# Expert layer: six buffers for row numbers, remainder tokens fetched as half rows, scatter-adds that skip empty slots

## The chip, the cores and the metric

The kernel runs on one core of a Trainium2 chip. A core has five engines that run in parallel, each with its own queue of instructions in program order: TensorE (PE: matmuls and transposes; PEld is its weight load), VectorE (DVE), ScalarE (ACT), GpSimd (POOL) and SyncE (SP, which here issues most DMAs). Sixteen DMA engines move data between DRAM and the on-chip memory SBUF. Indirect DMAs, whose rows are picked by a list of row numbers, are issued from POOL. The metric is the device time of one execution in microseconds.

## The reference, cut to what matters

One decoder layer for 1024 tokens with 1024 channels, in float32: token mixing by attention and a recurrence, cross-attention into 256 memory tokens, and a mixture of experts. Only the last part is changed:

```python
def grouped_moe(x, router_w, router_bias, w_gate, w_up, w_down):
    s = sigmoid(x @ router_w)                      # 16 experts in 4 groups of 4
    group = argmax(sum of the best two of s + router_bias in each group)
    e_idx = top_k(s + router_bias inside that group, 2)
    gate = s[e_idx] / sum(s[e_idx])
    # tokens sorted by expert, each expert's rows through
    y_rows = (silu(xb @ w_gate[e]) * (xb @ w_up[e])) @ w_down[e]   # 1024 -> 512 -> 1024
    return segment_sum(y_rows * gate, token)
x = layer_norm(DN_ALPHA * x + grouped_moe(x, ...), ln3_g, ln3_b)
```

With two experts to a token there are 2048 assignments. Which tokens an expert gets is known only while the kernel runs.

## The kernel before, in words

**Precision.** Each float32 operand of a large product is split into a high and a low part (`Ctx.split`, line 28: a cast on ACT, then a subtraction on DVE), and a product is three matmuls (`mm3`, lines 35 to 37): high x high, low x high, high x low.

**Lists.** The router writes, for every expert, a region of rows (token, 1, gate) in DRAM. An expert has 128 main slots (`CAP`); the eight experts with the most tokens (`NREM`) have 64 more (`REM`), their remainder. An empty slot's row is all zero. A loop behind the stage (`rest`) serves tokens past these slots.

**An expert.** Its weights come in six pieces of 1 MB (`load`, L1508, issued by SP), which are split by `parts`: the cast on ACT (L1517), the subtraction (L1518) for three of four parts on DVE, for one on POOL. `rows` (L1527 to L1535) loads 128 list rows `el` by SP and makes of them, on POOL, the tile `ef` (token, gate and intermediate values; `f` in the code) and the tile `eix` (`ix`: column 0 the row to read, column 1 the row to add to, which for an empty slot is a row past the tokens). `ef` and `eix` have three buffers each, for main lists and for remainders separately, so a fourth expert's list waits until the first one's last reader is done; for `eix` this is the scatter-add. `gather` (L1540) fetches the tokens' 1024 channels by an indirect DMA from `x2d` into `exg`. `turned` (L1547) transposes them, eight 128x128 transposes for 128 rows, into two banks of PSUM, which `split` turns into the stationary operand. For a remainder the 64 tokens are fetched twice, to both halves of the partitions, so that after the transposition 64 columns hold the high parts and 64 the low parts (`exr`).

The products with `w_gate` and `w_up` go through PSUM (`eacc`); for a remainder these are the matmuls of L1580. The hidden values are turned (L1547 for main tokens, `etq` L1599 for a remainder), multiplied (L1602, L1603 on DVE) and split (`ehh`, `ehl`; `ehr` for a remainder), and the product with `w_down` follows (lines 35 to 37; L1628 and L1629 for a remainder). ACT scales by the gate (L1616), and POOL adds the result to the sum `acc` in DRAM (`accd`) by an indirect DMA that accumulates (L1621): one of 128 rows for main tokens, two of 64 for a remainder. Every addition to `acc` waits for the one before it. The rows past the tokens (T to T + 127) take what empty slots give.

**Order.** `run` interleaves the stages of neighbouring experts: lists and main tokens of expert n + 2 are opened between the stages of n and n + 1, the remainder of n + 1 is fetched at the end. Experts with and without a remainder alternate from the second on. The queues' final order is a planner's, which simulates the engines and puts ready instructions first. The two experts at the end (`LATE`) fetch the sum so far, normalise their tokens and write them to the output by indirect DMAs with a bound on the row number (L1624). All other outputs come from `tiles` (L1757 to L1763), which loads `acc` by tiles, applies the last layer norm and stores.

Of the kernel before, what the change touches and what calls it, by code (L numbers as in the profile page):

```python
# [7 lines left out]
F32 = mybir.dt.float32  # L8
F32R = mybir.dt.float32r
I32 = mybir.dt.int32  # L10
AF = mybir.ActivationFunctionType
ALU = mybir.AluOpType
# [3 lines left out]
T, D = 1024, 1024  # L16
# [41 lines left out]
def load_xT(k, pool, ps, xin, ident, xh, xl, nt=NT, tag="xraw", bufs=3, pt=(("tp", 2),)):  # L58
    """four token tiles at a time: their loads, then their transposes"""
# [22 lines left out]
class Inproj:  # L82
    """x @ w_in; every consumer's layout goes to DRAM scratch."""
# [40 lines left out]
    # weights stationary, channels on the partitions  # L124
# [5 lines left out]
    def halves(self, wh, wl, evac, tag=None, marks=()):  # L130
        """a half of the tokens at a time"""
# [15 lines left out]
    def tokens(self, x, w, nh):  # L147
        """four token tiles by channels, from channels by tokens"""
        tp = self.bank(nh, "iptp")
        for i in range(4):  # L150
            self.k.nc.tensor.transpose(tp[:, w * i:w * i + w], x[:, 128 * i:128 * i + 128], self.ident[:w, :w])
        return tp[:, :4 * w]
# [112 lines left out]
def t5_onehot():  # L265
    """bucket of distance 1023 - i, one-hot (columns past distance 0 stay empty)"""
# [11 lines left out]
def bias_rows(k, pool, ev, ps, skew):  # L278
    """the bias by distance in DRAM, a copy for every partition; read with rows one place shorter, row p starts p places earlier"""
# [16 lines left out]
class Tables:  # L296
    """bias tables by distance: tb[p, h, c]: distance p + 896 - c; tcm: the compressed keys'; the window's far edge"""
# [24 lines left out]
def compress(k, cst, pool, ps):  # L322
    """k_cmp (twice on the partitions, in parts) and v_cmp (tokens on the partitions, in parts)"""
# [68 lines left out]
class Nsa:  # L392
    def __init__(self, k, cst, dp, skew, ps, keep, right):
        """first loads and the compressed branch's keys and values; ps: a pool with banks for that; keep: opens a pool that stays"""
# [33 lines left out]
    def load(self, t, g, half):  # L428
        """by halves of the tokens"""
# [10 lines left out]
    def attention(self):  # L440
# [6 lines left out]
        with tc.tile_pool(name="nq", reuse_waits="tile", bufs=1) as self.pq, tc.tile_pool(name="nw", reuse_waits="tile", bufs=2) as pw, tc.tile_pool(name="np", reuse_waits="tile", bufs=2, space=PSUM) as ps:  # L447
            def front(br, g, qt, t, st):
                """scores, softmax and gates of one tile of 128 queries of a group"""
# [28 lines left out]
            def weights(g, qt, sums, bs):  # L478
                """the gates over the sums"""
# [7 lines left out]
            def compressed(g, qt, t, st):  # L487
                """scores, softmax and gates against the compressed keys, four heads at once"""
# [20 lines left out]
            def back(g, qt, t, st):  # L509
                """all three branches into one sum: channels of four heads by queries"""  # L510
# [37 lines left out]
            def mix(a, na, b, nb):  # L548
                """steps of a among the first ones of b"""
# [71 lines left out]
class Rwkv:  # L621
    """RWKV-7 in chunks of 64 tokens; an item is a pair of heads and half of the tokens.

    Per chunk, with c the running sum of the log decay: al = e^{c_prev} kk, be = e^{-c} kk a, ka = e^{-c} k, rho = e^{c} r;
    U = (I + tril(al be^T, -1))^{-1} (al S^T + tril(al ka^T, -1) V); outputs and the next state are linear in S, U and V."""
# [37 lines left out]
    def low_rank(self):  # L663
        """the low-rank inputs past their nonlinearities, to DRAM"""
# [14 lines left out]
    def item(self, hp, n):  # L679
        """an item up to its maps, the end of the one before, the item's recurrence"""  # L680
# [12 lines left out]
    def steps(self, hp, n):  # L693
# [33 lines left out]
        # decay and in-context rate  # L727
# [12 lines left out]
        # normalised removal key  # L740
# [15 lines left out]
        # chunk operands: [al | rho | e^c at the chunk's end on a diagonal], and be, ka as a pair per chunk (swapped in odd chunks)  # L756
# [21 lines left out]
        # bonus  # L778
# [5 lines left out]
        # within the chunks  # L784
# [19 lines left out]
        # tokens on the partitions  # L804
# [22 lines left out]
        # inverses of the diagonal blocks of 32, a block to a partition  # L827
# [4 lines left out]
        # X (I + L^T) = I by rows: partition (row group of 8, block), a step clears one column to the right  # L832
# [16 lines left out]
        # (I + L)^-1 [al | L V], over both chunks of a unit  # L849
# [21 lines left out]
        # one map per chunk from the state to outputs and the next state  # L871
# [29 lines left out]
        # group norm, bonus, gate  # L901
# [34 lines left out]
EARLY = 4  # products of the merge during the attention before it  # L936
# [965 lines left out]
```

## Time and profile before

| what | value |
|---|---|
| runs, us | 1888.84, 1890.29, 1898.58 (median 1890.29) |
| profiled execution: span, us (its own time is given by this span alone) | 1889.9 |
| PE busy over the span | 1763.5 us, 93% |
| DVE busy | 1323.7 us, 70% |
| ACT busy | 849.3 us, 45% |
| POOL busy | 670.3 us, 35% |
| indirect and other POOL-issued DMAs (q0) | 26.62 MB, 5.7% of 16 engines' span |
| DMAs issued by SP (q1) | 273.59 MB, 44.7% |

The experts' matmuls begin at 1417.49 us of the span. Until 1444 the first expert runs almost alone, from 1444 to 1830 neighbouring experts overlap, and from 1830 on the last products, the last norm and the stores follow. Busy time is what an engine spent in instructions. A wait is put down to the instruction or DMA that released it. In the timeline a row has the start, the length in us, the engine, the line, the operation, output<-input, and in square brackets the idle time before it and what ended that.

### The profile page before, as it was taken

The page shows a single profiled execution, that of the slowest core. Times are in us where ns is not written, and L with a number is a line of the kernel's source. Part 1 is how long each engine was busy: PE and PEld are TensorE (multiplying, and loading weights), DVE is VectorE, ACT ScalarE, POOL GpSimd, SP SyncE. Part 2 cuts the span into 40 slices and gives each one's busy share as a digit, 9 for nine tenths or more (in the row PEclk, how much of TensorE's full clock was granted, in tenths as well). Part 3 has the DMA queues.
Part 4 walks back from the last instruction along what each step waited for, and adds up shares of the span by engine and source line. Part 5 has one row for each costly group of instructions (what it writes and reads, how often), then busy time and mean ns, then how long its engine had stood idle before and what let it go on. Part 6 is the DMA issues. An engine that isn't in the chain of part 4 may idle for free. (4 is left out here: it accounts for less than half of the span.)

```text
span 1889.9 us, 27421 instructions
## 1 busy us (share of the span) xinstructions
PE 1763.5 (93%) x9206; PEld 1433.0 (76%) x9206; DVE 1323.7 (70%) x2774; ACT 849.3 (45%) x1742; POOL 670.3 (35%) x756
## 2 busy tenths in 40 slices
PE   8999999999999999999999899999998999999992
PEld 6877777777788887877888577878796887787771
DVE  3225886888887512498987675557888788788876
ACT  4223313434333222287876341034415676666662
POOL 1123202221222122155445122100356665666556
PEclk9999999999999999999999999999989999999996
DMA  7363343444332227702101774033326999899984
GB/s 232 110 186 106 116 162 113 140 122 126 101 113 84 67 89 231 256 9 82 40 9 32 236 221 167 23 98 126 137 84 246 310 331 289 278 295 292 320 269 143
DMA packets 246144, 302.00 MB, mean 160 GB/s; under 512 B 54653, under 2 KB 142741, under 8 KB 245488
## 3 DMA queue, kind: packets, MB, share of 16 engines
q1 hardware_dynamic: 238016, 273.59, 44.7%
q0 software_dynamic: 7984, 26.62, 5.7%
q8 instruction: 74, 1.21, 0.3%
q14 instruction: 70, 0.57, 0.1%
HBM read 234.05 MB, written 70.98 MB: 161 GB/s over the span
## 5 line engine op out<-in xcount | busy, mean ns | idle before, releaser
L1518 DVE TENSOR_TENSOR wlo<-wraw,whi 128x512 fp32r<-128x512 f32 x288 | 274.5, 1000 | 34.9 <-ACT whi L1517 33.9
L35 PE MATMUL acc<-xh,wh 128*128 128x512 f32 (+1 forms) x656 | 273.0, 416 | 5.2 <-ACT wh L117 3.0
L37 PE MATMUL acc<-xh,wl 128*128 128x512 f32 (+1 forms) x656 | 267.0, 408 | 0.1
L36 PE MATMUL acc<-xl,wh 128*128 128x512 f32 (+1 forms) x656 | 267.1, 408 | 0.0
L1517 ACT CAST whi<-wraw 128x512 fp32r<-128x512 f32 x384 | 207.4, 621 | 36.5 <-PE eacc L1580 10.1
L118 POOL TENSOR_TENSOR wl<-wraw,wh 128x1024 fp32r<-128x1024 f32 (+1 forms) x41 | 104.0, 2536 | 304.1 <-ACT wh L117 259.8
L35 PEld LDWEIGHTS acc<-xh,wh 128*128 128x128 f32 (+1 forms) x656 | 125.0, 191 | 44.0 <-issue 6.8
L1518 POOL TENSOR_TENSOR wlo<-wraw,whi 128x512 fp32r<-128x512 f32 x96 | 138.8, 1476 | 49.4 <-ACT whi L1517 38.1
L37 PEld LDWEIGHTS acc<-xh,wl 128*128 128x128 f32 (+1 forms) x656 | 124.8, 190 | 33.8 <-issue 5.1
L36 PEld LDWEIGHTS acc<-xl,wh 128*128 128x128 f32 (+1 forms) x656 | 125.2, 191 | 30.0 <-issue 3.2
L840 DVE TENSOR_TENSOR tinv<-xinv,ln 128x248 f32<-128x248 f32 (+30 forms) x248 | 85.5, 345 | 40.5 <-DMA ln<-ld 24.3
L28 DVE TENSOR_TENSOR pl<-ptp,ph 128x512 fp32r<-128x512 f32 (+1 forms) x148 | 98.3, 681 | 11.6 <-ACT ph L28 11.1
L470 ACT ACTIVATE pp<-pp,nm 128x640 f32<-128x640 f32 (+7 forms) x128 | 94.2, 738 | 16.4 <-DVE nm L469 15.6
L28 ACT CAST ph<-ptp 128x512 fp32r<-128x512 f32 (+1 forms) x148 | 84.7, 582 | 26.6 <-PE ptp L523 23.6
L36 PE MATMUL eacc<-wlo,exh 128*128 128x512 f32 x240 | 94.2, 393 | 0.4 <-DVE wlo L1518 0.4
L35 PE MATMUL eacc<-whi,exh 128*128 128x512 f32 x240 | 94.3, 393 | 0.0
L37 PE MATMUL eacc<-whi,exl 128*128 128x512 f32 x240 | 94.1, 392 | 0.0
L841 DVE TENSOR_TENSOR xinv<-xinv,tinv 128x248 f32<-128x248 f32 (+30 forms) x248 | 87.6, 353 | 5.9
L475 POOL TENSOR_SCALAR pp<-pp,wgt 128x640 f32<-128x640 f32 (+7 forms) x128 | 88.9, 717 | 1.0
L969 POOL TENSOR_SCALAR lnrs<-lnmv 128x1 f32<-128x1 f32 x21 | 19.6, 934 | 181.0 <-DVE lnmv L968 173.1
L523 PE MATMUL ptp<-ident,pp 128*128 128x128 f32 x528 | 82.1, 278 | 0.3 <-DVE pl L28 0.3
L117 ACT CAST wh<-wraw 128x1024 fp32r<-128x1024 f32 (+1 forms) x41 | 42.2, 1030 | 81.8 <-PE acc L36 44.4
(498 smaller groups left out, 4476.2 us busy)
## 6 DMA issues: line engine op xcount, KB each, us to landing
wraw<-in_moe_w_up SPq DMA_DIRECT2D x32, 1024.0 KB
wraw<-in_moe_w_gate SPq DMA_DIRECT2D x32, 1024.0 KB
wraw<-in_moe_w_down SPq DMA_DIRECT2D x32, 1024.0 KB
wraw<-in_w_in SPq DMA_DIRECT2D x40, 512.0 KB
sm<-ev SPq DMA_DIRECT2D x32, 256.0 KB
sr<-ev SPq DMA_DIRECT2D x28, 256.0 KB
skew<-skew SPq DMA_DIRECT2D x1, 4608.0 KB
xraw<-in_x SPq DMA_DIRECT2D x8, 512.0 KB
```

The costliest lines, as they stand in the source:

```text
L28: x = nc.scalar.copy(hi, src), nc.vector.tensor_tensor(lo, src, hi.bitcast(F32), ALU.subtract)
L35: nc.tensor.matmul(out, ah, bh, start=start, stop=False)
L36: nc.tensor.matmul(out, ah, bl, start=False, stop=False)
L37: nc.tensor.matmul(out, al, bh, start=False, stop=stop)
L118: nc.gpsimd.tensor_tensor(wl, raw, wh.bitcast(F32), ALU.subtract)
L470: nc.scalar.activation(pt[:, :n], pt[:, :n], AF.Exp, bias=nm, scale=-1.0, accum_out=sums[:, 0, i:i + 1])
L475: nc.gpsimd.tensor_scalar(st[br, i][:, :n], st[br, i][:, :n], w[:, 0, i:i + 1], 1.0, ALU.mult, ALU.mult)
L523: nc.tensor.transpose(tp[:r, 128 * i:128 * i + 128], src, ident)
L840: nc.vector.tensor_tensor(tmp[:, :, :w], x[:, :, j:j + 1].to_broadcast([128, 8, w]), ln[:, j:j + 1, j + 1:].to_broadcast([128, 8, w]), ALU ...
L841: nc.vector.tensor_tensor(x[:, :, j + 1:], x[:, :, j + 1:], tmp[:, :, :w], ALU.subtract)
L1517: nc.scalar.copy(hi[:, cs], raw[:, cs])
L1518: (nc.gpsimd if i in LOPOOL else nc.vector).tensor_tensor(lo[:, cs], raw[:, cs], hi[:, cs].bitcast(F32), ALU.subtract)
```

## The change

Three edits, all in the expert layer. The constant tile `dum` gets a third column for the second one, 0 for the partitions 0 to 63 and 1 for 64 to 127. All other lines of the diff only blank comments and docstrings.

1. `ix` is no longer a tile of its own: it is columns 6 and 7 of `f`, which has eight columns and six buffers (`NROWS`) instead of three, for main lists and for remainders each.
2. A remainder's `gather` reads `x2d` as 2048 rows of 512 channels. The partitions 0 to 63 fetch the first half of their token's channels (row 2 x token), 64 to 127 the second half of the same tokens (row 2 x token + 1); one more POOL instruction makes this number. Four transposes instead of eight then give all channels in one bank, and one `split` instead of two writes `exr`.
3. The scatter-add has a bound on the row number, so that rows past the tokens are left out.

```diff
+NROWS = 6
-            "c_rows": rows, "c_dum": np.stack([dum, -dum], 1),
+            "c_rows": rows, "c_dum": np.stack([dum, -dum, (i >= 64).astype(np.float32)], 1),
...
-        f = pl.tile([128, 5], F32, tag="f" + tag, bufs=3, name="ef")
-        ix = pl.tile([128, 2], I32, tag="ix" + tag, bufs=3, name="eix")
+        f = pl.tile([128, 8], F32, tag="f" + tag, bufs=NROWS, name="ef")
+        ix = f[:, 6:8].bitcast(I32)
         for i in range(1, NLST):
             nc.gpsimd.tensor_tensor(f[:, 0:4], l[:, 0] if i == 1 else f[:, 0:4], l[:, i], ALU.add)
-        nc.gpsimd.tensor_copy(ix[:, 0:1], f[:, 0:1])
+        if twice:
+            nc.gpsimd.tensor_scalar(f[:, 5:6], f[:, 0:1], 2.0, self.dum[:, 2:3], ALU.mult, ALU.add)
+        nc.gpsimd.tensor_copy(ix[:, 0:1], f[:, 5:6] if twice else f[:, 0:1])
...
         xg = px.tile([128, D], F32, tag="xg" + tag, bufs=2 if tag == "m" else 1, name="exg")
+        if tag == "r":
+            xg, src = xg[:, :D // 2], self.x2d.rearrange("t (h d) -> (t h) d", h=2)
...
-            for q in range(2):
-                tp = self.turned(ps, rem[2], q).rearrange("p (c t) -> p c t", c=4)
-                k.split(tp[:, :, 0:64], xr[:, 4 * q:4 * q + 4, 0:64], xr[:, 4 * q:4 * q + 4, 64:128])
+            tp = self.turned(ps, rem[2], 0).rearrange("p (c h t) -> p c h t", c=4, h=2)
+            x4 = xr.rearrange("p (h c) t -> p c h t", h=2)
+            k.split(tp, x4[:, :, :, 0:64], x4[:, :, :, 64:128])
...
-                nc.gpsimd.indirect_dma_start(out=self.acc, ..., in_=y[r, :], in_offset=None, compute_op=ALU.add)
+                nc.gpsimd.indirect_dma_start(out=self.acc, ..., in_=y[r, :], in_offset=None, compute_op=ALU.add, bounds_check=T - 1, oob_is_err=False)
```

## Rows read from the trace of the kernel before

**Rows 1.** Stretch, length, busy us (instructions) of each engine, PE's clock, DMA share, GB/s.

```profile
1444.00:1830.00 386.00, 369.67 (x1761) 303.49 (x1760) 318.20 (x382) 257.49 (x494) 230.92 (x234) 0.99 0.93 296
1650.73:1655.05 4.32, 4.32 (x19) 3.76 (x20) 1.62 (x3) 1.46 (x3) 0.81 (x3) 0.60 0.89 261
```

**Rows 2.** Waits of PE, 1400 to 1890: us in total, times, longest us.

```profile
PE etp L1547 <- DMA exg<-x2d,eix: 13.7, 4, 5.0
...
PE eacc L1628 <- DVE ehr L28: 2.6, 5, 1.1
...
PE eacc L1580 <- DVE exr L28: 1.7, 1, 1.7
```

**Rows 3.** Waits of POOL, 1400 to 1890.

```profile
POOL eix L1532 <- DMA accd<-ey,eix: 32.2, 10, 4.7
POOL ef L1531 <- DMA el<-lst: 27.8, 10, 4.6
```

**Rows 4.** Timeline of POOL, 1643 to 1650.

```profile
1643.20 0.70 POOL L1532 CAST eix<-ef 128x1 int32<-128x1 f32 x1 [3.79 <-DMA accd<-ey,eix]
...
1644.18 1.48 POOL L1540 DMA_INDIRECT exg<-x2d,eix  x1 [0.16 <-POOL eix L1535]
1645.68 3.70 POOL L1518 TENSOR_TENSOR wlo<-wraw,whi 128x512 fp32r<-128x512 f32 x3
```

**Rows 5.** Timeline of PE at four remainders.

```profile
1598.07 0.50 PE L1628 MATMUL eacc<-whi,ehr 128*128 128x512 f32 x1 [0.22 <-DVE ehr L28]
...
1650.73 1.98 PE L1547 MATMUL etp<-ident,exg 128*128 128x128 f32 x12 [4.17 <-DMA exg<-x2d,eix]
1652.36 0.78 PE L1628 MATMUL eacc<-whi,ehr 128*128 128x512 f32 x1
...
1706.04 0.50 PE L1628 MATMUL eacc<-whi,ehr 128*128 128x512 f32 x1 [0.22 <-DVE ehr L28]
...
1757.53 2.80 PE L1547 MATMUL etp<-ident,exg 128*128 128x128 f32 x12 [2.98 <-DMA exg<-x2d,eix]
1759.98 0.78 PE L1628 MATMUL eacc<-whi,ehr 128*128 128x512 f32 x1
```

**Rows 6.** Timeline of DVE ahead of `ehr`.

```profile
1487.36 5.91 DVE L1518 TENSOR_TENSOR wlo<-wraw,whi 128x512 fp32r<-128x512 f32 x6
...
1645.99 3.69 DVE L28 TENSOR_TENSOR ehr<-etr,ehr 128x256 fp32r<-128x256 f32 x1 [0.47 <-ACT ehr L28]
...
1696.38 7.92 DVE L1518 TENSOR_TENSOR wlo<-wraw,whi 128x512 fp32r<-128x512 f32 x6
...
1757.77 0.42 DVE L28 TENSOR_TENSOR ehr<-etr,ehr 128x256 fp32r<-128x256 f32 x1 [0.47 <-ACT ehr L28]
```

**Rows 7.** Transposes of tokens: ns min/median/max, starts; eight in the chain.

```profile
L1547 PE MATMUL etp<-ident,exg x184: 270/273/475, 1428.3 to 1809.8; 128*128 128x128 f32 x184
...
1466.30 0.87 PE etp L1547 x8
```

**Rows 8.** Line 28 on DVE: a main half, a remainder's half (columns as before).

```profile
L28 DVE TENSOR_TENSOR exl<-etp,exh x30: 675/681/692, 1440.1 to 1812.1; 128x512 fp32r<-128x512 f32 x30
...
L28 DVE TENSOR_TENSOR exr<-etp,exr x16: 409/416/425, 1429.9 to 1778.1; 128x256 fp32r<-128x256 f32 x16
```

**Rows 9.** POOL's small step, its scatter-adds with landing, the bounded scatter.

```profile
L1533 POOL TENSOR_SCALAR ef<-ef,dum x24: 326/338/1827, 1422.0 to 1792.6; 128x1 f32<-128x1 f32 x24
...
L1621 POOL DMA_INDIRECT accd<-ey,eix x32: 1424/1696/2441, 1467.3 to 1870.3; - x32
...
DMA to landing us min/median/max: 4.9/8.0/10.9
...
L1624 POOL DMA_INDIRECT out<-exg,eix x2: 1037/1058/1078, 1872.7 to 1878.5; - x2
```

**Rows 10.** The first remainder: POOL's gather, PE's transposes.

```profile
1423.74 1.05 POOL L1540 DMA_INDIRECT exg<-x2d,eix  x1 [0.19 <-POOL eix L1535]
...
1428.32 1.97 PE L1547 MATMUL etp<-ident,exg 128*128 128x128 f32 x8 [5.01 <-DMA exg<-x2d,eix]
```

More of the change, by code (lines that the diff above doesn't have):

```diff
@@ L1466, in __init__ @@
         self.acc = dp.tile([T + 128, D], F32, name="accd")
-        self.dum, self.ii = p.tile([128, 2], F32, name="dum"), pw.tile([128, 64], F32, name="ii")
+        self.dum, self.ii = p.tile([128, 3], F32, name="dum"), pw.tile([128, 64], F32, name="ii")
         nc.sync.dma_start(self.dum, k.a["c_dum"])
@@ L1620, in result @@
                 ix = x[0][0:r.stop - r.start, 1:2]
-                nc.gpsimd.indirect_dma_start(out=self.acc, out_offset=bass.IndirectOffsetOnAxis(ap=ix, axis=0), in_=y[r, :], in_offset=None, compute_op=ALU.add)
+                nc.gpsimd.indirect_dma_start(out=self.acc, out_offset=bass.IndirectOffsetOnAxis(ap=ix, axis=0), in_=y[r, :], in_offset=None, compute_op=ALU.add, bounds_check=T - 1, oob_is_err=False)
             if late:
```

## The prediction

> **What bounds the kernel now.** I read the table of busy time by stretch first. The edits touch only the experts' stage, which fills the last fifth of the span. In its steady part, 386 us long, PE is busy for 369.7 us, DVE for 318.2, ACT for 257.5, POOL for 230.9, and the DMA engines for 93% [rows 1]. So PE sets the pace there, and only two things can shorten this stretch: less work on PE, or fewer of its 16 idle microseconds. What happens on POOL counts only as far as PE waits for it.
>
> Next come the waits of PE. The largest is for tokens that an indirect DMA fetches: 13.7 us in 4 waits. A second kind is smaller and regular, L1628 waiting for `ehr`, the split hidden values of a remainder [rows 2]. Then the waits of POOL: 32.2 us in 10 waits, all at L1532, where a row number is written into `ix` and the scatter-add that read this buffer three experts earlier has not landed; and 27.8 us at L1531 for the list rows themselves [rows 3]. A third view, POOL's instructions in order of time, joins the two. L1532 is held for 3.79 us until 1643.20, and the gather behind it can go out only at 1644.18 [rows 4]. PE then sits idle for 4.17 us until those tokens are there at 1650.73 [rows 5]. So a buffer number on POOL reaches PE through the gather. The waits of PE name no weight load, so the 93% of the DMA engines is not what PE waits for.
>
> **The change part by part.** The page gives the profiled execution by its span, 1889.9 us; that is 0.4 us under the median of the three runs, 1890.3, so I subtract from the median.
>
> *Six buffers for the row numbers.* With a distance of six experts instead of three, L1532 of the experts' main lists finds a scatter-add that was issued three experts earlier still. All 32.2 us of this wait go from POOL [rows 3]. What that is worth is read at the places where PE pays. There are three kinds.
>
> At 1650 the gather would go out 3.8 us sooner, and PE's 4.17 us would shrink to 0.4. But L1628, next on PE, needs `ehr`, which DVE ends only at 1645.99 + 3.69 = 1649.68 [rows 6]. So L1628 moves from 1652.36 to 1649.75 at the best that DVE allows: 2.6 us. After the idle time PE's granted clock is 0.60 for 4.32 us, between its two levels of 1.2 and 2.4 GHz [rows 1]; the part behind 1652.36 is 2.69 us, and at full clock 40% of it, 1.1 us, would not be needed. Together 3.7 us; with `ehr` earlier too it would be at most 4.17 + 0.4 x 4.32 = 5.9.
>
> At 1757 PE waits 2.98 us, and L1628 starts at 1759.98 [rows 5]; `ehr` is ready at 1757.77 + 0.42 = 1758.19 [rows 6]. I take the difference, 1.8 us; at most 2.98 plus the stretching of twelve transposes (2.45 us to L1628 where 12 x 0.109 = 1.3 would do [rows 5, 7]), 4.1.
>
> At 1597 and 1704 the gather's lateness is nearly covered: L1628 waits for `ehr` right behind the transposes [rows 5], and `ehr` is late because DVE's six subtractions ahead of it took 7.92 us at 1696, beside POOL's three, where the same six took 5.91 us at 1487 [rows 6]. If POOL comes to its three sooner, at most that difference of 2.0 us is won at each place, and nothing at all if DVE is held just as long. I take half, 1.0 each.
>
> The term is 3.7 + 1.8 + 2.0 = 7.5 us, between 0 and 14.0. What is late next: `ehr` on DVE, and on POOL the list rows at L1531, which stay as they are, since their loads stand on SP's queue between weight loads that this change leaves alone. No wait is added. The gather moves ahead on POOL's queue, past nothing but the time it was held.
>
> *Remainders by halves.* Eight experts have a remainder. Each now needs 4 transposes instead of 8. Back to back eight take 0.87 us, 0.109 each [rows 7]; the duration of one, 273 ns, overlaps the next. For seven experts that is 28 x 0.109 = 3.1 us off PE's own work, at most 28 x 0.273 = 7.6. The splits become one of 128x512 instead of two of 128x256: 0.68 against 0.83 us on DVE [rows 8], and likewise on ACT. Neither bounds, so the saving counts nothing; but the last part is ready 0.68 - 0.42 = 0.27 us later on DVE and somewhat later on ACT, some 0.5 us. PE waited for this split once, for 1.7 us [rows 2]. I take 0, with 7 x 0.5 = 3.5 us lost or 1.7 gained as the ends. The cover is the other expert's matmuls between the transposes and L1580.
>
> The first expert's remainder is the one gather that nothing covers: PE idles 5.01 us before 1428.32 [rows 10]. Its row number needs one more POOL instruction, nearest L1533 at 0.34 us [rows 9]; half the bytes land sooner; four transposes at the low clock go (0.98 of the 1.97 us), but ACT and DVE must then split all of it before L1580, where the second half had been split beside PE. I set these against each other at 0, between 0.5 lost and 2.0 gained. The Trainium skill, in "DMA: Bandwidth & Descriptors", section "Anatomy of one DMA", fits such a DMA as about 2.0 us plus bytes over 436 GB/s; an estimate by the Trainium skill's fit is 0.6 us less for 256 KB, and the sum would be 12.2 in place of the one below. From issue to first use this gather took 4.6 us here [rows 10], where the Trainium skill's fit has 3.2 for 512 KB, so its fixed part is too small for this place.
>
> In the steady part the extra instruction adds 8 x 0.34 = 2.7 us to POOL, up to 8 x 1.83 [rows 9]. POOL's idle 155 us hide it [rows 1], and a remainder's gather goes out many microseconds before its use.
>
> *Scatter-adds that skip empty slots.* There are 16 x 128 + 8 x 64 = 2560 slots for 2048 assignments, so 512 are empty if nobody overflows. A main slot is added once, a remainder's slot twice (two partial sums), so 512 to 1024 of 3072 added rows go, 17 to 33%. The bound check as such is on the late output scatter already: 1.06 us, not longer than the 1.70 of the additions [rows 9]. I take no POOL cost. Landing of an addition is 4.9 us at the shortest and 8.0 in the middle [rows 9]. Inside the stage no PE wait hangs on it once the buffers are six. At the end two additions in a row, which must follow each other, stand ahead of the last norm's loads of `acc`: 2 x 0.17 x (8.0 - 4.9) = 1.0 us gained, between 0 and 2 x 0.33 x 8.0 = 5.3.
>
> **Sum:** 7.5 + 3.1 + 0 + 1.0 = 11.6 us, so 1890.3 - 11.6 = 1878.7 us. All lower ends give 3.1 - 3.5 - 0.5 = 0.9 us slower, all upper ends 14.0 + 7.6 + 1.7 + 2.0 + 5.3 = 30.6 faster.
>
> **Rivals.** *Small: DVE, not the gather.* L1628 waits for `ehr` in five waits already [rows 2]. If the freed POOL holds DVE as long as now, or if POOL stops at L1531 for its lists instead [rows 3], the first term shrinks to the 2.6 us of the 1650 passage or less; with 3.1 for transposes some 5 us remain: 1885. It is also the time if the six buffers don't take the wait away, say because the row number now lies in the same tile as the gate, which ACT reads late. Against it stands the direct chain at 1650, where gather and PE follow each other.
>
> *Large.* Every stall ends, `ehr` included, and the smaller transfers shorten the additions: 14.0 + 3.1 + 1.7 + 2.0 + 3 = 24, so 1866. For it: DMA engines are 93% busy [rows 1], and all three edits take load from them. Against: L1628's own waits are not touched.
>
> *Slower: POOL's subtractions meet DVE's short chain.* At 1645.68 POOL ran three subtractions of weights, 3.70 us, and DVE's `ehr`, which began at 1645.99, took 3.69 us where 0.42 is usual; both end within 0.3 us of each other [rows 4, 6]. The place is L1602, L1603 and `ehr` ahead of L1628, once for each remainder; the price is 3.69 - 0.42 = 3.3 us each time POOL's run falls there. Freed from its wait, POOL runs at other times than now. If it meets this chain in all seven steady passages, PE loses 23 us against 11.6 gained: 1902. It decides from four passages on (11.6 / 3.3 = 3.5). Against: POOL is delayed now, and that is what bunches its three subtractions; earlier ones must still wait for ACT's casts one by one. The Trainium skill has the rule, in "SBUF — State Buffer", section "SBUF: two separate sides": a GpSimd instruction and a DVE instruction with two SBUF inputs hold one port pair in turn, for a whole instruction. By that rule each subtraction of POOL may hold DVE for its own length, and the trace agrees with 3.69 us at 1645.99.
>
> **How the numbers follow.** Half a per cent, 9.45 us, is what a measurement of this kernel can tell from no change. The forecast's case, 1873 to 1884, has 0.50; the large one 0.15, the small one 0.23, the slower one 0.12. About two thirds of the forecast's case lie below 1880.8, 0.33; with the large case faster has 0.48. Of the slower case 0.09 lies above 1899.7 and 0.03 within. The rest, 0.17 + 0.23 + 0.03 = 0.43, is no change. The range runs from 1866, the large case, to 1893, which leaves out most of the slower one.
>
> **What would show it.** Right, if L1532's waits for `accd` are gone from POOL, etp<-exg counts 184 - 32 = 152 transposes, the gathers of main tokens go out with their list rows, and PE's waits for exg shrink to the first one. Wrong, if PE waits as long as before with `ehr` or the lists named instead; if L1580's waits for exr grow to several microseconds; or if the stretch from 1444 to 1830 keeps its length although the 32 us are gone.

## Result: the change makes the kernel slower

The changed kernel takes 1910.03 us (median of 9 runs, 1902.70 to 1916.79), the kernel before 1894.14 us (9 runs beside them): ratio 1.0083, 95% interval 1.0054 to 1.0112. The prediction was 1878.7 us, some 0.6% faster, with a range up to 1893. It is wrong in its sign.

The profiled execution of the changed kernel has a span of 1908.9 us, 19.0 more than that of before. The experts' first product starts at 1430.5 us there and at 1417.5 before, so 13.0 of the 19 arise ahead of the experts, where the two programs have the same instructions in the same order. The first experiment below shows that this part is not the change's. From the first to the last product of an expert it is 449.8 us against 444.3 before and 433.8 in a second profile of before. Against that second profile the stage is 16.0 us longer, which is the whole difference of the medians (15.9).

What the change does is seen first. POOL's own DMAs move 20.67 MB instead of 26.62, and the transposes of tokens are 152 instead of 184 [rows 7] (operation, times, ns min/median/max, first and last start). Of the changed kernel, page and tile view:

```profile
q0 software_dynamic: 7472, 20.67, 4.5%
```

```profile
L1553 PE MATMUL etp<-ident,exg x152: 270/273/421, 1439.4 to 1832.2; 128*128 128x128 f32 x152
L1546 POOL DMA_INDIRECT exg<-x2d,ef x23: 990/1048/1515, 1436.0 to 1809.3; - x23
```

The waits of PE in the changed kernel (us in total, times, longest), which answer to [rows 2]:

```profile
PE eacc L37 <- DVE ehl L28: 15.2, 7, 4.0
PE eacc L35 <- ACT ehh L28: 5.9, 2, 5.2
PE etq L1605 <- DVE egr L1587: 4.4, 4, 2.3
PE etp L1553 <- DMA exg<-x2d,ef: 3.1, 1, 3.1
PE eacc L36 <- POOL wlo L1519: 2.6, 2, 1.5
PE etp L1553 <- DVE exl L28: 1.7, 1, 1.7
```

The waits for `exg` are gone but for the first remainder, as predicted. In their place PE waits for VectorE: for `ehl`, the low part of the hidden values, and for `egr`, the copy of a remainder's products. POOL's waits, which answer to [rows 3]:

```profile
POOL ef L1532 <- DMA el<-lst: 78.2, 15, 9.4
POOL wlo L1519 <- ACT whi L1518: 41.5, 24, 4.6
```

The 32.2 us at the row numbers have gone; the wait for list rows has grown from 27.8 to 78.2 us. The steady stretch, which answers to [rows 1], and one low-clock stretch (length, busy us of PE, PEld, DVE, ACT, POOL, PE's clock, DMA share, GB/s):

```profile
1457.00:1843.00 386.00, 367.73 (x1702) 300.93 (x1701) 320.46 (x369) 250.73 (x476) 219.48 (x235) 0.97 0.89 282
1611.67:1615.09 3.42, 3.42 (x10) 2.65 (x9) 3.42 (x7) 0.69 (x1) 0.00 (x0) 0.50 1.02 374
```

PE is idle for 18.3 us of 386 (16.3 before), and its clock is 0.97 instead of 0.99. Four of the five new waits of over 2 us are followed by a clock of 0.50, the lower of its two levels (1.2 of 2.4 GHz), three times for 3.4 us and once for 10.2 us. The second row is enough to see the price: a wait of 2.2 us is paid almost twice. From 30 to 400 us behind the first product PE is idle for 17.9 us at a mean clock of 0.97, and in the second profile of before for 8.2 us at 1.00: 9.7 us more of waits and, an estimate from these rows, 0.03 x 370 = 11 us by the clock.

The next three views show one place of the changed kernel: VectorE, POOL and PE up to 1611 us (start, length, instruction, and in brackets the idle time before).

```profile
1594.87 0.67 DVE L1596 SCALAR_TENSOR_TENSOR eth<-eth,eacc 128x512 f32<-128x512 f32 x1
1595.47 9.50 DVE L1519 TENSOR_TENSOR wlo<-wraw,whi 128x512 fp32r<-128x512 f32 x5
1604.89 0.68 DVE L1587 COPY egr<-eacc 128x512 f32<-128x512 f32 x1
1605.49 3.58 DVE L1519 TENSOR_TENSOR wlo<-wraw,whi 128x512 fp32r<-128x512 f32 x4
1608.99 0.68 DVE L1574 SCALAR_TENSOR_TENSOR eth<-eth,eacc 128x512 f32<-128x512 f32 x1
1609.59 0.68 DVE L28 TENSOR_TENSOR ehl<-etp,ehh 128x512 fp32r<-128x512 f32 x1
```

```profile
1586.66 0.72 POOL L1532 TENSOR_TENSOR ef<-el 128x4 f32<-128x4 f32 x1 [6.67 <-DMA el<-lst]
...
1589.94 1.29 POOL L1519 TENSOR_TENSOR wlo<-wraw,whi 128x512 fp32r<-128x512 f32 x1
...
1591.90 1.29 POOL L1519 TENSOR_TENSOR wlo<-wraw,whi 128x512 fp32r<-128x512 f32 x1
...
1596.01 1.30 POOL L1519 TENSOR_TENSOR wlo<-wraw,whi 128x512 fp32r<-128x512 f32 x1
1597.48 1.92 POOL L1627 DMA_INDIRECT accd<-ey,ef  x1 [0.17 <-issue]
1598.85 4.36 POOL L1519 TENSOR_TENSOR wlo<-wraw,whi 128x512 fp32r<-128x512 f32 x3
```

```profile
1605.62 1.10 PE L1605 MATMUL etq<-ii,egr 128*128 128x64 f32 x8 [0.46 <-DVE egr L1587]
...
1610.33 0.50 PE L37 MATMUL eacc<-whi,ehl 128*128 128x512 f32 x1 [2.22 <-DVE ehl L28]
```

VectorE needs 9.50 us for five subtractions. Undisturbed, six take 3.70 us (a view of the last experiments, below), 0.62 each. POOL runs four of its own, 1.30 + 4.36 = 5.66 us, in the same stretch: 5 x 0.62 + 5.66 = 8.8, nearly all of the 9.50. So the two engines do not subtract at the same time. Taken one by one, three of the five last 0.68 us, one lasts 2.40 us, beside POOL's single one, and one 5.37 us, across POOL's three that follow each other without a gap:

```profile
1598.40 5.37 DVE L1519 TENSOR_TENSOR wlo<-wraw,whi 128x512 fp32r<-128x512 f32 x1
```

So it matters whether POOL's subtractions stand in a bunch. Ahead of this one POOL stood still for 6.67 us until list rows came at 1586.66; then follow two lists and six subtractions with hardly a gap. That the wait makes the bunch is read from this view and was not tried by itself. `egr`, `eth` and `ehl` stand behind VectorE's subtractions in its queue, and PE stops for them. Two experts on, at 1649.51, five subtractions of VectorE take 9.51 us again.

### The profile page after: what moved, and what is told of

Read it like the earlier page. It is cut to its first block, busy times and chain, and to the rows that moved or that the text cites. A ratio compares the mean times of both kernels' runs of the same rounds, so it can differ in the third digit from the quotient of the medians.

```text
span 1908.9 us, 27381 instructions
## 1 busy us (share of the span) xinstructions
PE 1770.8 (93%) x9174; PEld 1436.9 (75%) x9174; DVE 1329.2 (70%) x2766; ACT 848.7 (44%) x1734; POOL 668.3 (35%) x764
## 3 DMA queue, kind: packets, MB, share of 16 engines
q0 software_dynamic: 7472, 20.67, 4.5%
## 4 chain that ended last, share of the span: by engine, by line
PE 43%; DVE 15%; DMA 8%; issue 5%; ACT 2%; SPq 1%; POOL 1%; DVEq 0%; ACTq 0%; POOLq 0%
DVE wlo L1519 4%; PE ptp L523 3%; PE eacc L37 3%; PE eacc L35 3%; PE eacc L36 3%; PE acc L35 2%; PE acc L36 2%; PE acc L37 2%; PE o L538 2%; PE o L537 2%; PE eacc L1586 2%; PE sp L461 2%; PE sp L463 2%; PE wacc L37 2%; PE wacc L36 2%
## 5 line engine op out<-in xcount | busy, mean ns | idle before, releaser
L1519 DVE TENSOR_TENSOR wlo<-wraw,whi 128x512 fp32r<-128x512 f32 x288 | 283.9, 1040 | 34.1 <-ACT whi L1518 33.9
L840 DVE TENSOR_TENSOR tinv<-xinv,ln 128x248 f32<-128x248 f32 (+30 forms) x248 | 91.3, 368 | 42.5 <-DMA ln<-ld 26.2
L470 ACT ACTIVATE pp<-pp,nm 128x640 f32<-128x640 f32 (+7 forms) x128 | 94.3, 738 | 16.7 <-DVE nm L469 15.9
L841 DVE TENSOR_TENSOR xinv<-xinv,tinv 128x248 f32<-128x248 f32 (+30 forms) x248 | 81.2, 327 | 5.9
L898 ACT COPY state<-rseq 64x64 f32<-64x64 f32 x128 | 26.7, 209 | 116.8 <-PE rseq L894 97.8
```

Source lines behind the costliest of these rows:

```text
L470: nc.scalar.activation(pt[:, :n], pt[:, :n], AF.Exp, bias=nm, scale=-1.0, accum_out=sums[:, 0, i:i + 1])
L840: nc.vector.tensor_tensor(tmp[:, :, :w], x[:, :, j:j + 1].to_broadcast([128, 8, w]), ln[:, j:j + 1, j + 1:].to_broadcast([128, 8, w]), ALU ...
L841: nc.vector.tensor_tensor(x[:, :, j + 1:], x[:, :, j + 1:], tmp[:, :, :w], ALU.subtract)
L1519: (nc.gpsimd if i in LOPOOL else nc.vector).tensor_tensor(lo[:, cs], raw[:, cs], hi[:, cs].bitcast(F32), ALU.subtract)
```

## The experiments

All ratios are against the kernel before, run beside each; 95% intervals in brackets. "Stage" is the time from the first to the last product of an expert in the profile, "steady idle" PE's idle time from 30 to 400 us behind the first product.

**The control and the single edits.** Four kernels: before once more (its tile `ef` has a sixth column that nothing uses); six buffers alone; the halves alone; the bound alone. In short:

```diff
 a2: -bufs=3, name="ef"  +f[:, 6:8] as ix, bufs=NROWS
 a3: +2 * token + half, half-row gather, one split
 a4: -compute_op=ALU.add)
     +compute_op=ALU.add, bounds_check=T - 1, oob_is_err=False)
```

> The kernel before once more, as a control: nothing of the change is in it, and its instructions stand in the order of before on every engine. Of the 19.0 us between the profiled executions of before and after, 13.0 lie ahead of the first product of an expert, in a stretch whose instructions are the same and in the same order. If those 13 are a drift from one execution to the next, this profile's first product of an expert may lie anywhere from 1417 to 1431 us, with the median time within 0.4% of before. If they belong to the change, this one's first product lies within 3 us of before's 1417.5 and the ratio is 1.000 +- 0.003.

Measured: 1.0002 [0.9973, 1.0030]. The first product came at 1429.1 us, 11.6 later than in the first profile of before, whose instructions are the same in the same order: the 13 us ahead of the experts are drift between executions. More than that, the stage was 433.8 us and not 444.3, since most of the waits that the prediction was built on were not there:

```profile
PE etp L1548 <- DMA exg<-x2d,eix: 5.3, 2, 4.9
```

13.7 us in four waits [rows 2] were 5.3 in two, of which 4.9 is the first remainder. Steady idle is 8.2 us against 15.6.

> The row numbers' six buffers alone; remainders are fetched as before and additions as before. Theory 'order': with other buffers the planner writes another order of instructions on VectorE, TensorE, ScalarE and GpSimd, and the order costs the time; then this kernel has VectorE's weight subtractions ahead of the subtraction that makes ehl, TensorE waits of over 2 us for ehl, and a ratio of 1.002 to 1.009, with the exg waits of [rows 2] gone all the same. Rival 'edits': six buffers are no cost, the gain of [rows 2] comes through, ratio 0.995 to 0.998, and the loss is in the halves (one more GpSimd operation a remainder) or the bounded additions. Rival 'drift': ratio as in the control, whatever the experts do.

Measured: 1.0102 [1.0060, 1.0144], stage 453.4 us. The waits for `exg` have gone, those for `ehl` are 24.3 us in 8. The planner did write another order on TensorE, VectorE, ScalarE and GpSimd; in SP's queue one small load changed its place. By itself this edit loses as much as the three together.

> The halves of a token's channels alone: the remainder's gather takes 256 KB less, four transposes and one split less, one more GpSimd operation; three buffers of row numbers and unbounded additions as before. Theory 'order': its order differs from before's as well, from the first expert's remainder on; ratio 1.002 to 1.009 if weight subtractions come ahead of ehl here, else 0.997 to 1.000. Rival 'edits': 28 transposes less give 3.1 us, the additional operation on GpSimd takes up to 8 remainders x 1 us of its time, ratio 0.998 to 1.003 by the edit itself.

Measured: 1.0054 [1.0031, 1.0078], stage 447.7. Its loss is of another kind: `ehl` costs 6.0 us, but PE waits 16.3 us in 7 for `exg`, and once 9.4 us for `eth` near the end. A second profile of this kernel, for which it was expected:

> A second profile of the halves alone in the planner's own order (1.0054 before): theory 'order' expects gathers' waits of TensorE for exg again at four or more of the remainders, each 1.4 to 2.4 us, and a long wait for eth (9.4 us in the first profile) near 1860 us if that belongs to the order; if it was a passing thing, it is under 3 us here.

gave seven waits for `exg` (18.1 us) and 9.1 us for `eth` at the same place. Both come again with this order.

> The bounded additions alone. The instructions stand in the order of before on every engine, so that this one shows the edit itself: theory 'order' expects 0.999 to 1.001 (1 us at the end at most); rival 'edits' allows up to 1.004 if the check of the bound on GpSimd's queue costs something on each of 32 additions, seen as longer issues of the additions and later ends of the row's traffic to accd.

Measured: 0.9955 [0.9929, 0.9980], stage 430.0. Both theories missed this gain of 8.5 us. The order is that of before on every engine, so it is the edit's own. POOL's DMAs move 22.77 MB instead of 26.62, which at 4 KB a row is 940 of 3072 rows, within the 512 to 1024 of the prediction. The tail behind the last product is no shorter (28.7 us, 27.8 before). About half of the gain can be seen at one place, some 400 us behind the first product. There VectorE stops for the first load of the sum `acc` (`lnst`, for the last norm), with an `ehl` behind it in its queue; SP issues that load when an addition has landed, 5.0 us behind the addition's issue before and 3.1 with the bound. Before, VectorE and PE, then the bound alone:

```profile
DVE lnst L967 <- DMA wraw<-accd: 6.2, 1, 6.2
PE eacc L37 <- DVE ehl L28: 6.8, 2, 4.1
```

```profile
DVE lnst L967 <- DMA wraw<-accd: 2.1, 1, 2.1
PE eacc L37 <- DVE ehl L28: 4.2, 1, 4.2
```

In all four profiles in the order of before without the bound VectorE waits 6.2 to 8.0 us here, and PE 2.0 to 3.5 us for that `ehl`, with 3.4 us at the lower clock at this place; in the three with the bound and all the work VectorE waits 1.9 to 2.2 us and PE not at all. By an estimate from these rows that is 2.0 to 3.5 us and up to 1.7 us for the clock. Where the rest comes from is not settled.

**The edits in the order of before.** Each engine's instructions of the experts' stage are held in the order that they have in the kernel before, by edges that only order instructions of one engine and add no wait between engines. In short:

```diff
+def hold(tc):
+    for e, steps in PLAN:    # an engine, the places of its instructions in the program in the order wanted
+        ins = instructions of engine e
+        for a, b in pairs(steps):
+            tc.add_manual_dep(ins[b], ins[a].name, NoSync)
...
+                    hold(tc)
                     ex.rest()
```

> The six buffers of row numbers, with every engine's instructions held in the order of the kernel before (each instruction of the experts' stage is made to follow the one that precedes it there; order on all five engines the same as before, no wait added between engines). The planner's own order for this edit measured 1.0102, with an experts' stage (first to last product) of 453.4 us against 433.9 us in the control. Theory 'order': the ratio falls to 0.997 to 1.002, the stage to 430 to 436 us, no ehl wait of over 0.5 us before 1825 us, exg waits no longer than the control's. Rival 'edits' (row numbers that are read from one tile with the gates, or converted early, cost something themselves): the ratio stays above 1.006 and the stage above 445 us.

Measured: 0.9974 [0.9957, 0.9991], stage 431.4, no wait for `ehl` ahead of the tail, `exg` only at the first remainder.

> All three edits, every engine's instructions in the order of before: the four transposes and the one split of a remainder stand where the first half's stood, the additional operation on GpSimd just ahead of the conversion that reads it. Theory 'order': none of the loss is the edits', the bounded additions' 0.9955 comes through, ratio 0.990 to 0.998 and an experts' stage of 425 to 433 us. Rival 'edits': above 1.003, with the loss that the halves alone showed (1.0054).

Measured: 0.9944 [0.9925, 0.9963], 1882.51 us, stage 424.0. The same three edits gain 0.56% in this order and lose 0.83% in the planner's, some 26 us apart. PE's waits (lines are 3 further down in this file):

```profile
PE eacc L38 <- ACT ehh L31: 5.6, 2, 4.9
PE etp L1556 <- DMA exg<-x2d,ef: 4.5, 1, 4.5
PE eacc L1589 <- DVE exr L31: 4.3, 3, 2.4
PE eacc L40 <- DVE ehl L31: 4.3, 1, 4.3
PE eacc L1637 <- DVE ehr L31: 3.1, 7, 1.2
```

The waits for `ehh` and `ehl` are those of the last expert, which before has too. VectorE at the place that answers to 1595 us above:

```profile
1587.47 0.67 DVE L1599 SCALAR_TENSOR_TENSOR eth<-eth,eacc 128x512 f32<-128x512 f32 x1
1589.33 1.29 DVE L1522 TENSOR_TENSOR wlo<-wraw,whi 128x512 fp32r<-128x512 f32 x2 [1.18 <-ACT whi L1521]
1590.67 0.69 DVE L1590 COPY egr<-eacc 128x512 f32<-128x512 f32 x1
1591.28 2.86 DVE L1522 TENSOR_TENSOR wlo<-wraw,whi 128x512 fp32r<-128x512 f32 x4
1596.82 0.69 DVE L1577 SCALAR_TENSOR_TENSOR eth<-eth,eacc 128x512 f32<-128x512 f32 x1 [2.68 <-ACT eth L1576]
1597.42 0.68 DVE L31 TENSOR_TENSOR ehl<-etp,ehh 128x512 fp32r<-128x512 f32 x1
```

Two subtractions stand between `eth` and `egr`, not five, and VectorE waits for the work (2.68 us) instead of PE for VectorE.

**Which engine's order.** Six buffers, with POOL's and SP's order of before and the others' of the planner; then the counterpart.

> Six buffers; GpSimd's and the load queue's order that of before, TensorE, ScalarE and VectorE held in the order that the planner wrote for this edit (ratio of that order 1.0102). It tells which part of the order costs. If it is the products' chain (the copy of egr ahead of the split of ehh on ScalarE, the transposes of eth behind all sixteen exr products on TensorE, subtractions of weights ahead of ehl on VectorE), the ehl waits stay near 24 us in 8 waits and the ratio at 1.006 to 1.011. If it is GpSimd, which stops for lists that it meets early (91.7 us in 14 waits there, 16.7 us in the control) and is late with its share of the weights, the ratio falls to 0.998 to 1.003 and the ehl waits below 8 us.

Measured: 1.0253 [1.0226, 1.0281]. Neither theory had this: PE waits 5 to 7 us for `exg` at every second expert from 1555 us on, as if its new order wanted the tokens earlier than POOL's old order fetches them.

> The counterpart: six buffers; TensorE, ScalarE and VectorE in the order of before, GpSimd and the load queue in the order that the planner wrote for this edit. If the products' chain costs, the ratio falls to 0.997 to 1.003 though GpSimd still waits over 60 us for lists; if GpSimd's waits cost, the ratio stays at 1.005 to 1.011 and TensorE waits for wlo or for what VectorE has behind them.

Measured: 1.0168 [1.0142, 1.0193], POOL waits 88.9 us for lists. Its two parts have to be kept apart: the stage is 452.8 us, as with the whole new order (453.4), and the rest of the loss lies behind the last product (41.5 us to the end, 28.1 with the whole new order). VectorE's subtractions last 1048 ns on average here and 1046 with the whole new order, but 985 in the order of before and also in the swap ahead of this one. So POOL's order sets how long VectorE's subtractions last, though VectorE has its old order here; and POOL's old order beside the others' new one is slower still by another wait, that for tokens. What each engine's order costs can't be added up from such swaps.

**Lists earlier.** The first cause that is left to try: POOL stops for list rows that it meets too early. In short:

```diff
-                main, rem = self.list(r, s0)    # in open_(n)
+            while len(toks) <= min(n + 1, NE - 1):
+                lists(len(toks))                # the lists of n + 1, in open_(n)
...
-tag="l" + tag, bufs=2, name="el"
+tag="l" + tag, bufs=3, name="el"
```

> All three edits in an order of the planner's own, but each expert's list rows are opened one expert (some 25 us) earlier, with three buffers el instead of two; the gathers stay where they are in the program. From the second expert's remainder on, TensorE, VectorE and ScalarE stand in the same order as in the changed kernel (1.0083); GpSimd's and the load queue's differ by the lists' places. Theory 'lists': the changed kernel loses because its order counts on list rows that in fact land 7 to 8 us after their issue, so that GpSimd stops for them (78.2 us in 15 waits) with weight subtractions and gathers behind it; with the lists early these waits fall below 20 us, the ehl waits before 1830 us below 3 us in all, and the ratio to 0.992 to 1.000. Rival 'chain': the places of eth's transposes and of ehl behind weight subtractions cost by themselves; the list waits go and the ratio stays at 1.004 to 1.010.

Measured: 1.0057 [1.0036, 1.0079]. The list waits fell to 42.5 us in 11 only, and PE waits for `exl` instead, 16.4 us in 6. Its VectorE and its PE at one such place:

```profile
1607.40 10.52 DVE L1519 TENSOR_TENSOR wlo<-wraw,whi 128x512 fp32r<-128x512 f32 x6
```

```profile
1618.91 1.11 PE L1553 MATMUL etp<-ident,exg 128*128 128x128 f32 x4 [4.70 <-DVE exl L28]
```

Six subtractions in 10.52 us, with five of POOL's (6.38 us) beside them: the same meeting, ahead of another step.

**The halves in the order of before.**

> The halves of a token's channels alone, in the order of before on every engine (its own order measured 1.0054). By the working of the prediction, 28 transposes at 0.109 us are 3.1 us and the splits and the additional operation cost nothing: 0.997 to 0.9995. By difference of the runs so far (all three 0.9944, six buffers 0.9974, bounded additions 0.9955, so 1.0015 would be left for the halves) 1.000 to 1.003. Theory 'edit': the additional operation and the single split cost by themselves, above 1.003.

Measured: 1.0007 [0.9987, 1.0026]. The 28 transposes give nothing that can be told from zero here; with three buffers PE again waits 12.6 us in 4 for `exg`.

**VectorE's short steps first.** The planner's order of the changed kernel, but with `eth`, `egr`, `etr`, `ehl`, `exl`, `exr` and `ehr` two, then four subtractions earlier in VectorE's queue.

> The changed kernel in the order that the planner wrote for it, except that on VectorE, from the second expert to the third from the end, every short step (eth, egr, etr, ehl, exl, exr, ehr) stands two weight subtractions earlier; the other engines' order is that of the changed kernel. Theory 'VectorE behind': in the changed kernel a subtraction lasts 1.04 us on average where the shortest takes 0.67, VectorE is behind when a short step is due, and TensorE waits for ehl (15.2 us), egr (4.4) and exl (1.7); with two subtractions less ahead (some 2 us) the regular waits of 2.2 us for ehl go and the ratio falls to 0.998 to 1.004. Rival 'TensorE's chain': the order on TensorE and ScalarE (all sixteen exr products ahead of eth's transposes, the copy of egr ahead of ehh) leaves too little between a step and its use; the ratio stays at 1.005 to 1.011.

> The same with four subtractions instead of two (some 4 us). Theory 'VectorE behind': ratio 0.994 to 1.001, no wait for ehl over 1 us before 1830 us, unless weights come late in turn, which would be seen as waits of TensorE for wlo. Rival 'TensorE's chain': 1.005 to 1.011 as before.

Measured: 1.0109 [1.0091, 1.0128] and 1.0175 [1.0160, 1.0191], waits of 26.8 us for `ehl` and 25.4 us for `exl`. The theory that these steps merely stand too far back in VectorE's queue has fallen. VectorE and POOL in the second of them:

```profile
1666.97 10.90 DVE L1522 TENSOR_TENSOR wlo<-wraw,whi 128x512 fp32r<-128x512 f32 x6
```

```profile
1668.06 6.85 POOL L1522 TENSOR_TENSOR wlo<-wraw,whi 128x512 fp32r<-128x512 f32 x5
```

POOL's order is unchanged, and five of its subtractions now meet six of VectorE's.

**The meeting itself.** POOL's weight subtractions are left out, first in the planner's order, then in that of before.

```diff
-            (nc.gpsimd if i in LOPOOL else nc.vector).tensor_tensor(lo[:, cs], ...)
-        return hi, lo
+            if i not in LOPOOL:
+                nc.vector.tensor_tensor(lo[:, cs], ...)
+        return hi, Low(hi, lo)    # reads hi where POOL's part would be
```

> All three edits in the planner's order of the changed kernel; GpSimd's quarter of the weights' low parts is not computed (the high part is read in its place, so the output is not the reference's), all other instructions stand as there. Theory 'meeting': without GpSimd's subtractions VectorE's last 0.68 to 0.75 us on average instead of 1.04, the waits for ehl and egr before 1830 us (18 us) fall below 4, and the kernel comes within 4 us of e2: ratio 0.988 to 0.996. Rival 'TensorE's chain': the waits stay over 10 us, the ratio at 1.002 to 1.010 and the distance to e2 at 12 us or more.

> The same leaving out, with every engine in the order of before (with GpSimd's subtractions this order measured 0.9944). TensorE had some 3 us of waits left in the steady part there, so little is to be had: 0.990 to 0.995 by both theories; it is the measure for e1.

Measured: 0.9880 [0.9847, 0.9912], 1871.15 us, and 0.9863 [0.9837, 0.9889], 1867.99 us. The two orders, some 26 us apart with POOL's subtractions (1.0083 and 0.9944), are 3.2 us apart without them. In the planner's order the profile then lists no wait of PE between 1440 and 1811 us, though POOL waits longer for lists than in the changed kernel (101.7 us, 78.2). TensorE's own order, which is that of the changed kernel here, costs nothing then, so the rival of the two expectations before has fallen as well. VectorE's subtractions there (busy us, mean ns, then idle time before):

```profile
L1531 DVE TENSOR_TENSOR wlo<-wraw,whi 128x512 fp32r<-128x512 f32 x282 | 181.0, 688 | 44.2 <-ACT whi L1529 43.6
```

In the changed kernel the same 282 are 277.9 us, 1040 ns each.

**All on VectorE.** VectorE's 282 subtractions cost it 277.9 - 181.0 = 97 us more beside POOL's 94. In that time it can do those 94 itself.

```diff
-CUT, LOPOOL = 4, (2,)
+CUT, LOPOOL = 4, ()
```

> All three edits; VectorE computes all four quarters of the weights' low parts, GpSimd none, in the planner's own order. VectorE then has 376 subtractions of 0.69 us (the mean without GpSimd's beside them), 259 us, against 282 of 1.04 = 293 us in the changed kernel; so it should be no busier and TensorE's waits for ehl and egr go. Theory 'meeting': ratio 0.985 to 0.997. Rival: VectorE with a third more instructions is late all the same, as when its short steps stood behind more subtractions; ratio above 1.003, waits for ehl or exl over 10 us.

Measured: 0.9914 [0.9882, 0.9946], 1884.94 us, all the work done, in an order of the planner's own. VectorE's subtractions, POOL's waits and a run of six:

```profile
L1519 DVE TENSOR_TENSOR wlo<-wraw,whi 128x512 fp32r<-128x512 f32 x376 | 232.5, 684 | 29.3 <-ACT whi L1518 29.3
```

```profile
POOL ef L1532 <- DMA el<-lst: 114.5, 15, 16.9
```

```profile
1600.77 3.70 DVE L1519 TENSOR_TENSOR wlo<-wraw,whi 128x512 fp32r<-128x512 f32 x6
```

376 subtractions take less of VectorE's time than 282 beside POOL's. In spite of POOL's 114.5 us for lists PE waits for tokens only twice ahead of the last experts, 2.32 us at the first remainder and 2.46 at 1468.09 us. The second is behind a meeting of another kind: twenty subtractions of VectorE without a gap, and two small steps of POOL, 0.2 and 0.3 us in the median, that end only behind them:

```profile
1450.49 12.11 DVE L1519 TENSOR_TENSOR wlo<-wraw,whi 128x512 fp32r<-128x512 f32 x20
1450.36 12.28 POOL L1539 CAST ef<-ef 128x1 int32<-128x1 f32 x1
1450.54 12.33 POOL L1535 TENSOR_SCALAR ef<-ef,dum 128x1 f32<-128x1 f32 x1
```

> The kernel before with the same single change: all weight subtractions on VectorE, planner's own order, none of the three edits. Theory 'meeting': in the order of before the meeting hardly reached TensorE, so 0.993 to 1.002, with the waits for row numbers and tokens as before (up to 8 us in the steady part), and f1 is 5 to 12 us faster than this one.

Measured: 1.0103 [1.0071, 1.0134], 1918.61 us. It was expected near 1. Without the edits the same line of code loses, and the views say where: with POOL free of subtractions, POOL waits for row numbers and PE for tokens.

```profile
POOL eix L1533 <- DMA accd<-ey,eix: 65.8, 12, 7.8
```

```profile
PE etp L1548 <- DMA exg<-x2d,eix: 23.5, 7, 5.6
```

Here the edits, with the order that the planner gives them, are worth 33.7 us (1918.61 to 1884.94).

**Which edits the version needs.** Six buffers and the bound, without the halves, in the order of before.

> Six buffers and bounded additions without the halves, every engine in the order of before. The product of the single runs is 0.9974 x 0.9955 = 0.9929; with the halves 0.9944 was measured. If the halves give nothing of their own (1.0007 in the order of before), this one lies at 0.991 to 0.996 and is as good as all three; if their 28 transposes and 256 KB a remainder count once the waits for tokens are gone, it lies at 0.996 to 0.999.

Measured: 0.9929 [0.9914, 0.9945], 1885.20 us, stage 424.7, steady idle 4.9 us. It is as good as all three edits in this order (0.9944). This one, all three in this order, and all three with VectorE alone (0.9914) beat both kernels; their intervals overlap.

## Why the prediction was wrong

**The step that failed** is the passage under the six buffers: "since their loads stand on SP's queue between weight loads that this change leaves alone. No wait is added. The gather moves ahead on POOL's queue, past nothing but the time it was held." It priced each edit inside the order of before. What it says of SP's queue holds but for one load. But the order is a planner's output, and the buffers were one of its inputs: with six of them it writes a new order for the other four engines. POOL's subtractions then come more often in bunches (six of three or more without a gap, one with the same edits in the old order), VectorE stands still beside them, and PE waits for VectorE, 15.2 us for `ehl` and 4.4 for `egr`. The same edits in the old order gain 10.6 us (0.9944 of 1894 us), and in the new one lose 16.

**Its signs.** All four signs of being right came true (no wait of POOL for `accd` at the row numbers, 152 transposes, main tokens fetched right behind their lists, PE waiting for `exg` at the first remainder alone), and the kernel is slower. They showed that the edits do what they were meant to, not that nothing else moves. Of the signs of being wrong, the waits on other names came nearest, but they named `ehr` and the lists, and PE waits for `ehl` and `egr`.

**The sum by its own terms, in the order of before.** Together they were predicted at 11.6 us and measured at 10.6 (7.0 to 14.2). Six buffers: 7.5 predicted, 4.9 measured (1.7 to 8.1). Halves: 3.1 predicted, 1.3 lost measured (4.9 lost to 2.5 gained), so the whole 3.1 isn't there while tokens are waited for; and since six buffers with the bound (0.9929) are no slower than all three (0.9944), no run shows a gain from the halves. Bounded additions: 1.0 predicted, 8.5 measured (3.8 to 13.4), the term that was mis-sized most. Its reason, that inside the stage no wait of PE hangs on an addition, was wrong: the wait for `ehl` some 400 us behind the first product hangs on one, by way of VectorE. The first term lies within its interval, but it rested on one execution: the waits for `exg` that it starts from were 13.7 us there, 5.3 in the control and 12.6 with the halves in the order of before. That the sum of the three comes within 1.0 us of the measured one is in part luck: a term of 3.1 that isn't seen and one that is 7.5 too small.

**The rivals.** The slower one named the mechanism, POOL's subtractions beside VectorE's, with 1902 us and a chance of 0.12. Its place was wrong: it looked at `etr` and `ehr`, and the price falls on the runs of weight subtractions ahead of `egr`, `eth`, `ehl` and `exl`. One meeting was priced at 3.3 us; at 1595 us it costs VectorE 9.50 - 5 x 0.62 = 6.4, of which PE pays 0.46 + 2.22 in waits and some 1.7 by the lower clock behind them. The Trainium skill, "SBUF — State Buffer", section "SBUF: two separate sides", says of a VectorE instruction with two SBUF inputs and a GpSimd one that reads SBUF that whichever starts first holds the shared ports for its whole instruction. The sums 8.8 against 9.50 us and, in the kernel with early lists, 6 x 0.62 + 6.38 = 10.1 against 10.52 agree with it. Here the holding went on over several instructions in a row, over POOL's three (5.37 us for one of VectorE's) and over VectorE's twenty (12.3 us for POOL's small steps). The argument against this rival, that earlier subtractions of POOL must still come one by one behind ACT's casts, didn't hold: at 1595 us POOL runs its subtractions without a wait for ACT, whose casts are already there.

**What stays open.** How much of the loss each engine's order makes. Where the other half of the bound's 8.5 us comes from. And the kernel with early lists and that with the halves have mean subtractions no longer than before's (984 and 987 ns, 999 before) and lose all the same. The long ones tell a little more: subtractions of over 4 us are 7 in the changed kernel, 6 with six buffers alone, 4 and 2 in the two profiles of before, and none with six buffers or with all three edits in the order of before; but they are 3 with early lists and 1 with the halves. So it also matters what waits behind a meeting. That this explains the halves' waits for `exg` too was not tried.

## What to carry to other kernels

Where a planner orders the queues, a change of a buffer count can change the whole program: compare the order of the instructions before you price the edit, and to learn what an edit is worth hold the old order. Before a wait is taken away, see what the freed engine will run, and beside whom. Elementwise work that POOL took from VectorE was no help in the changed kernel: with 94 of 376 subtractions on POOL VectorE spent more time on its 282 than on all 376 alone. In the kernel before, giving them back to VectorE lost 1.0% all the same, with another order and waits for row numbers and tokens.

## What the runs showed of the hardware

The first product of an expert lay between 1417.5 and 1439.0 us in twenty profiles, whatever the kernel, and PE's waits for `exg` differed between two profiles of before by 8 us. A single profile of this kernel can't carry a term of 5 us. At one place list rows of 2 KB, issued between weight loads of 1 MB on the same queue, were used 7 to 8 us after their issue, POOL waiting for them (two loads from 1657.75 us on, used at 1665.67 in the kernel with six buffers alone). A subtraction of VectorE, 0.62 us in a run of its own, lasted 5.37 us beside three of POOL in a row, and a POOL step of 0.2 us (median) lasted 12.28 us beside twenty of VectorE in a row. A bound on the row number of an accumulating DMA took no time from POOL: the additions last 1.65 us (median) with it and 1.70 without [rows 9].
